# Batched experts MLP: program order on every engine, with the next expert's x cast and transposed between the two layers

## The chip, the cores and the metric

The kernel runs on one core of a Trainium2 chip. The metric is the device time of one execution in microseconds (us). TensorE (PE in the rows, its weight loads PEld) does the matrix products and the transposes, VectorE (DVE) and ScalarE (ACT) move results out of PSUM and cast, GpSimd (POOL) issues the loads of the weights, SyncE (SP) issues the loads of x and the stores of the output. The DMA engines that all these transfers share are shown as "DMA".

## The reference

There are eight experts. Each has its own 256 rows of x, its own first weight matrix and its own second one, all in float32:

```python
n_experts, capacity, hidden, expert_hidden = 8, 256, 512, 2048
x:  (8, 256, 512)    w1: (8, 512, 2048)    w2: (8, 2048, 512)
h = np.matmul(x, w1)
h = np.maximum(h, 0)
return np.matmul(h, w2).astype(np.float32)
```

## The kernel before

Write L1(e) for the first layer of expert e, L2(e) for the second, w1(e) and w2(e) for their weights, T(e) for the cast and transposition of x(e), out(e) for the result. The experts are numbered 0 to 7.

The weights are cast to bfloat16 by the DMA on the way in: each w1(e) and each w2(e) is one tile of 2 MB in SBUF, loaded by one DMA from GpSimd (lines 54 and 60), except that the last, w2(7), comes in four pieces. There are four buffers for w1 and four for w2. A DMA of x(e) (line 50) and one of out(e) (line 117) move 512 KB each and are issued by SyncE; out(7) goes in two halves, one by SyncE (line 114), one by ScalarE (line 115).

T(e) is three steps: ScalarE casts x(e) to bfloat16 (line 64), TensorE does 8 transposes into PSUM (line 68), VectorE copies them to SBUF (line 72). L1(e) is 64 matmuls of 256 columns (line 79) in 8 groups; after each group the ReLU moves the result to SBUF, on ScalarE (line 89) and VectorE (line 87) in turn. L2(e) is 32 matmuls of 512 columns into two PSUM tiles (line 103), then one copy on VectorE (line 111) and one on ScalarE (line 112), and the store.

The program lists the layers in this order, and the weights are requested in the same order: L1(0), L2(0), L1(1), L2(1), ... up to L1(4), L2(4), and then

```python
order += [(1, e) for e in range(E - 3, E)] + [(2, e) for e in range(E - 3, E)]
```

that is L1(5), L1(6), L1(7), L2(5), L2(6), L2(7). T(e) stands at the head of `first_layer(e)`. But what an engine issues first is not taken from this text: the framework's scheduler traces the whole program with its dependencies and buffers, and decides with a model of its own in which order each engine gets its instructions. Each engine then runs its list strictly in order, waiting at an instruction whose inputs are not there.

Of the kernel before, what the change touches and what calls it, by code (L numbers as in the profile page):

```python
# [1 line left out]

# [5 lines left out]


@with_exitstack  # L10
def kernel(
    ctx: ExitStack,
    tc: tile.TileContext,
    x: bass.AP,
    w1: bass.AP,
    w2: bass.AP,
    out: bass.AP,
):
    nc = tc.nc
    P = 128  # L20
    bf = mybir.dt.bfloat16
    f32 = mybir.dt.float32

    E, C, H = x.shape
    F = w1.shape[2]
    MT = C // P
    KT1 = H // P
    KT2 = F // P
    AHEAD = 4


    x_r = x.rearrange("e (p mt) k -> e p mt k", p=P)
    w1_r = w1.rearrange("e (p kt) n -> e p kt n", p=P)
    w2_r = w2.rearrange("e (p kt) n -> e p kt n", p=P)
    out_r = out.rearrange("e (p mt) n -> e p mt n", p=P)

    const = ctx.enter_context(tc.tile_pool(name="const", bufs=1))
    wpool = ctx.enter_context(tc.tile_pool(name="weights", bufs=4))
    xpool = ctx.enter_context(tc.tile_pool(name="xs", bufs=AHEAD))
    tpool = ctx.enter_context(tc.tile_pool(name="xts", bufs=2))  # L40
    hpool = ctx.enter_context(tc.tile_pool(name="hidden", bufs=4))
    opool = ctx.enter_context(tc.tile_pool(name="outs", bufs=3))
    ps_h = ctx.enter_context(tc.tile_pool(name="ps_h", bufs=4, space=bass.MemoryType.PSUM))
    ps_o = ctx.enter_context(tc.tile_pool(name="ps_o", bufs=4, space=bass.MemoryType.PSUM))

    x_sb, w1_sb, w2_sb, ht = {}, {}, {}, {}

    def load_x(e):
        x_sb[e] = xpool.tile([P, MT, H], f32, tag="x", name="x_sb")
        nc.sync.dma_start(x_sb[e][:], x_r[e])  # L50

    def load_w1(e):
        w1_sb[e] = wpool.tile([P, KT1, F], bf, tag="w1", name="w1_sb")
        nc.gpsimd.dma_start(w1_sb[e][:], w1_r[e])  # L54

    def load_w2(e):
        w2_sb[e] = wpool.tile([P, KT2, H], bf, tag="w2", name="w2_sb")
        cuts = (0, KT2) if e < E - 1 else (0, 6, 11, 14, 16)
        for lo, hi in zip(cuts, cuts[1:]):
            nc.gpsimd.dma_start(w2_sb[e][:, lo:hi, :], w2_r[e, :, lo:hi, :])  # L60

    def first_layer(e):
        x_bf = tpool.tile([P, MT, H], bf, tag="xb", name="x_bf")
        nc.scalar.copy(x_bf[:], x_sb[e][:])  # L64
        pt = ps_o.tile([P, KT1, MT, P], bf, tag="ps_o", name="pt_tr")
        for kt in range(KT1):
            for mt in range(MT):
                nc.tensor.transpose(  # L68
                    pt[:, kt, mt, :], x_bf[:, mt, kt::KT1], identity[:]
                )  # L70
        xt = tpool.tile([P, KT1, C], bf, tag="xt", name="xt_sb")
        nc.vector.tensor_copy(xt[:], pt[:].rearrange("p k m q -> p k (m q)"))  # L72

        ht[e] = hpool.tile([P, KT2, C], bf, tag="ht", name="ht_sb")
        for g in range(KT2 // 2):
            ph = ps_h.tile([P, 2, C], f32, tag="ps_h", name="pt_h")
            for i in range(2):
                for kt in range(KT1):
                    nc.tensor.matmul(  # L79
                        ph[:, i, :],  # L80
                        w1_sb[e][:, kt, 2 * g + i::KT2],
                        xt[:, kt, :],
                        start=(kt == 0),
                        stop=(kt == KT1 - 1),
                    )
            if g % 2:
                nc.vector.tensor_relu(ht[e][:, 2 * g:2 * g + 2, :], ph[:])  # L87
            else:
                nc.scalar.activation(  # L89
                    ht[e][:, 2 * g:2 * g + 2, :], ph[:],  # L90
                    mybir.ActivationFunctionType.Relu,
                )

    def second_layer(e):
        last = e == E - 1
        po = [
            ps_o.tile([P, H], f32, tag="ps_o", name=f"pt_o{mt}") for mt in range(MT)
        ]
        order = [(kt, mt) for kt in range(KT2) for mt in range(MT)]
        if last:  # L100
            order = order[:-4] + [(kt, mt) for mt in range(MT) for kt in (KT2 - 2, KT2 - 1)]
        for kt, mt in order:
            nc.tensor.matmul(  # L103
                po[mt][:],
                ht[e][:, kt, mt * P:(mt + 1) * P],
                w2_sb[e][:, kt, :],
                start=(kt == 0),
                stop=(kt == KT2 - 1),
            )
        o = opool.tile([P, MT, H], f32, tag="o", name="out_sb")  # L110
        nc.vector.tensor_copy(o[:, 0, :], po[0][:])  # L111
        nc.scalar.copy(o[:, 1, :], po[1][:])  # L112
        if last:
            nc.sync.dma_start(out_r[e, :, 0, :], o[:, 0, :])
            nc.scalar.dma_start(out_r[e, :, 1, :], o[:, 1, :])
        else:
            nc.sync.dma_start(out_r[e], o[:])


    order = []  # L120
    for e in range(E - 3):
        order += [(1, e), (2, e)]
    order += [(1, e) for e in range(E - 3, E)] + [(2, e) for e in range(E - 3, E)]

    for e in range(AHEAD):
        load_x(e)
    for layer, e in order:
        (load_w1 if layer == 1 else load_w2)(e)
        if (layer, e) == (1, 0):
            identity = const.tile([P, P], bf, name="identity")  # L130
            make_identity(nc, identity)
    for layer, e in order:
        if layer == 1:
            first_layer(e)
        else:
            second_layer(e)
            if e + AHEAD < E:
                load_x(e + AHEAD)


# [1 line left out]
_INS = ['x', 'w1', 'w2']  # L142
_OUTS = [((8, 256, 512), 'float32')]


# [23 lines left out]
```

## Time and profile before

| what | value |
|---|---|
| time, median of 3 runs (lowest to highest) | 193.09 us (192.41 to 193.12) |
| time of the profiled execution | 193.58 us |
| its span, first to last instruction | 191.8 us |
| PE busy | 130.0 us, 68% |
| DVE, ACT, POOL busy | 32.7, 33.0, 10.8 us |
| mean granted TensorE clock | 0.922 |
| HBM read | 71.30 MB, 394 GB/s over the span |

The span runs from the first to the last instruction; the time of the same execution is 1.78 us longer. Times in the rows count from the start of the span. The granted clock is a share of full speed: 1.00 is 2.4 GHz and 0.50 is 1.2 GHz. The largest busy share of an engine, 68%, belongs to PE; the line of the DMA engines has to be read beside it.

### The profile page before, as it was taken

The numbers are of one execution on the slowest core, as the hardware profiler recorded it, in microseconds if no ns is written. First come the engines' busy times: TensorE is split into PE (matmuls) and PEld (weight loads), VectorE is DVE, ScalarE is ACT, GpSimd is POOL, SyncE is SP. The second block draws the span as 40 slices with busy tenths as digits, with TensorE's granted clock in tenths as the row PEclk, the third lists the DMA queues.
The fourth block names the chain that finished last, engine by engine and source line by source line (L and its number), as shares of the span: only waits on it lengthen the run. The fifth ranks groups of instructions, "written<-read, shape, count | busy, mean of one in ns | idle before, by whom it ended". The sixth has DMA issues, their size and how long they took to land.

```text
span 191.8 us, 1891 instructions
## 1 busy us (share of the span) xinstructions
PE 130.0 (68%) x824; PEld 91.5 (48%) x832; DVE 32.7 (17%) x48; ACT 33.0 (17%) x49; POOL 10.8 (6%) x25
## 2 busy tenths in 40 slices
PE   0204969489591978669492956998395029999990
PEld 0103854269240874349341942488385017944440
DVE  0100220203102140204102220053024001301100
ACT  4202220313002220312103220043022001301101
POOL 7200010100100010000301101010000000000000
PEclk9999999969999699969999997899879856999997
DMA  7999999999999999999999899999999999998113
GB/s 253 220 220 259 220 259 222 256 218 260 214 264 214 263 212 263 215 256 221 253 220 262 206 262 222 219 198 256 224 220 215 219 219 219 204 209 212 45 66 111
DMA packets 5192, 42.06 MB, mean 219 GB/s; under 512 B 576, under 2 KB 576, under 8 KB 3264
## 3 DMA queue, kind: packets, MB, share of 16 engines
q0 software_dynamic: 2736, 33.56, 82.4%
q1 hardware_dynamic: 2304, 8.13, 11.2%
q10 hardware_dynamic: 144, 0.26, 0.4%
q8 instruction: 6, 0.10, 0.2%
q14 instruction: 2, 0.02, 0.0%
HBM read 71.30 MB, written 4.19 MB: 394 GB/s over the span
## 4 chain that ended last, share of the span: by engine, by line
PE 54%; DMA 24%; another core or an unknown queue 17%; POOL 1%; issue 1%; DVE 0%; ACT 0%; POOLq 0%; ACTq 0%
PE pt_o L103 27%; PE pt_h L79 26%; DMA w_sb<-in_w_dram 24%; PE pt_tr L68 1%; POOL w_sb L54 0%; DVE xt_sb L72 0%; ACT out_sb L112 0%; POOL w_sb L60 0%; POOL identity masks.py:199 0%; POOL identity masks.py:197 0%; POOLq masks.py:199 0%; ACTq L112 0%; POOLq L153 0%
## 5 line engine op out<-in xcount | busy, mean ns | idle before, releaser
L79 PE MATMUL pt_h<-xt_sb,w_sb 128*128 128x256 bf16 x512 | 67.7, 301 | 29.7 <-DMA w_sb<-in_w_dram 29.4
L79 PEld LDWEIGHTS <-w_sb 128*128 128x128 bf16 x512 | 61.7, 149 | 35.9 <-DMA w_sb<-in_w_dram 30.8
L103 PE MATMUL pt_o<-w_sb,ht_sb 128*128 128x512 bf16 x248 | 58.4, 391 | 22.2 <-DMA w_sb<-in_w_dram 21.6
L103 PEld LDWEIGHTS <-ht_sb 128*128 128x128 bf16 x256 | 25.6, 100 | 52.9 <-issue 25.6
L87 DVE TENSOR_SCALAR ht_sb<-pt_h 128x512 bf16<-128x512 f32 x32 | 22.1, 692 | 87.1 <-PE pt_h L79 87.1
L89 ACT ACTIVATE ht_sb<-pt_h 128x512 bf16<-128x512 f32 x32 | 19.1, 597 | 72.0 <-PE pt_h L79 72.0
L112 ACT COPY out_sb<-pt_o 128x512 f32<-128x512 f32 x8 | 4.7, 586 | 68.7 <-PE pt_o L103 68.7
L111 DVE COPY out_sb<-pt_o 128x512 f32<-128x512 f32 x8 | 5.5, 692 | 61.3 <-PE pt_o L103 61.3
L64 ACT CAST x_bf<-x_sb 128x1024 bf16<-128x1024 f32 x8 | 8.4, 1045 | 13.3 <-DMA x_sb<-in_x_dram 13.3
L54 POOL DMA_DIRECT2D w_sb<-in_w_dram x8 | 4.5, 559 | 77.0 <-PE pt_h L79 76.2
L68 PE MATMUL pt_tr<-identity,x_bf 128*128 128x128 bf16 x64 | 5.1, 231 | 5.1 <-ACT x_bf L64 5.1
L60 POOL DMA_DIRECT2D w_sb<-in_w_dram x11 | 5.9, 542 | 39.0 <-DMA w_sb<-in_w_dram 23.1
L68 PEld LDWEIGHTS <-x_bf 128*128 128x128 bf16 x64 | 4.6, 117 | 6.2 <-ACT x_bf L64 5.1
L72 DVE COPY xt_sb<-pt_tr 128x1024 bf16<-128x1024 bf16 x8 | 5.4, 688 | 6.2 <-PE pt_tr L68 6.2
L64 ACT ACT_TABLE_LOAD x1 | 1.3, 1283 | 0.7 <-PEq L153 0.7
masks.py:199 POOL TENSOR_SCALAR_AFFINE_SELECT identity<-identity 128x128 bf16<-128x128 bf16 x1 | 0.3, 312 | 0.1
masks.py:197 POOL MEMSET identity<- 128x128 bf16 x1 | 0.2, 223 | 0.0
L153 POOL MEMSET const-float32-0.0<- 128x1 f32 x1 | 0.1, 99 | 0.2 <-issue 0.2
L153 POOL MEMSET const-bfloat16-1.0<- 128x1 bf16 x1 | 0.1, 102 | 0.0
L153 POOL MEMSET const-uint8-127<- 128x1 uint8 x1 | 0.1, 102 | 0.0
L153 POOL MEMSET const-float32-1.0<- 128x1 f32 x1 | 0.1, 99 | 0.0
## 6 DMA issues: line engine op xcount, KB each, us to landing
w_sb<-in_w_dram POOLq DMA_DIRECT2D x15, 2048.0 KB, 66.2
x_sb<-in_x_dram SPq DMA_DIRECT2D x8, 512.0 KB, 30.3
out_dram<-out_sb SPq DMA_DIRECT2D x7, 512.0 KB, 15.7
w_sb<-in_w_dram POOLq DMA_DIRECT2D x1, 768.0 KB, 68.2
w_sb<-in_w_dram POOLq DMA_DIRECT2D x1, 640.0 KB, 67.3
w_sb<-in_w_dram POOLq DMA_DIRECT2D x1, 384.0 KB, 58.1
w_sb<-in_w_dram POOLq DMA_DIRECT2D x1, 256.0 KB, 49.6
out_dram<-out_sb SPq DMA_DIRECT2D x1, 256.0 KB, 2.4
```

The lines of the kernel that those rows point to most:

```text
L54: nc.gpsimd.dma_start(w1_sb[e][:], w1_r[e])
L60: nc.gpsimd.dma_start(w2_sb[e][:, lo:hi, :], w2_r[e, :, lo:hi, :])
L64: nc.scalar.copy(x_bf[:], x_sb[e][:])
L68: nc.tensor.transpose(pt[:, kt, mt, :], x_bf[:, mt, kt::KT1], identity[:])
L72: nc.vector.tensor_copy(xt[:], pt[:].rearrange("p k m q -> p k (m q)"))
L79: nc.tensor.matmul(ph[:, i, :], w1_sb[e][:, kt, 2 * g + i::KT2], xt[:, kt, :], start=(kt == 0), stop=(kt == KT1 - 1),)
L87: nc.vector.tensor_relu(ht[e][:, 2 * g:2 * g + 2, :], ph[:])
L89: nc.scalar.activation(ht[e][:, 2 * g:2 * g + 2, :], ph[:], mybir.ActivationFunctionType.Relu,)
L103: nc.tensor.matmul(po[mt][:], ht[e][:, kt, mt * P:(mt + 1) * P], w2_sb[e][:, kt, :], start=(kt == 0), stop=(kt == KT2 - 1),)
L111: nc.vector.tensor_copy(o[:, 0, :], po[0][:])
L112: nc.scalar.copy(o[:, 1, :], po[1][:])
L153: nc = _bacc.Bacc("TRN2", target_bir_lowering=False, num_devices=1)
```

## The change

The scheduler is switched off: with `tc.manual_schedule()` every engine issues its instructions in the order of the program text. T(e) becomes a function of its own, `transpose_x`. It is called for expert 0 before the loop, and for expert e + 1 right behind L1(e). The layers, the loads and the buffers stay as they were.

```diff
-    x_sb, w1_sb, w2_sb, ht = {}, {}, {}, {}
+    x_sb, w1_sb, w2_sb, xt, ht = {}, {}, {}, {}, {}
+    ctx.enter_context(tc.manual_schedule())
...
-    def first_layer(e):
+    def transpose_x(e):
         x_bf = tpool.tile([P, MT, H], bf, tag="xb", name="x_bf")
         nc.scalar.copy(x_bf[:], x_sb[e][:])
...
-        xt = tpool.tile([P, KT1, C], bf, tag="xt", name="xt_sb")
-        nc.vector.tensor_copy(xt[:], pt[:].rearrange("p k m q -> p k (m q)"))
+        xt[e] = tpool.tile([P, KT1, C], bf, tag="xt", name="xt_sb")
+        nc.vector.tensor_copy(xt[e][:], pt[:].rearrange("p k m q -> p k (m q)"))
 
+    def first_layer(e):
         ht[e] = hpool.tile([P, KT2, C], bf, tag="ht", name="ht_sb")
...
+    transpose_x(0)
     for layer, e in order:
         if layer == 1:
             first_layer(e)
+            if e + 1 < E:
+                transpose_x(e + 1)
         else:
             second_layer(e)
             if e + AHEAD < E:
                 load_x(e + AHEAD)
```

On TensorE, near the end of the program, this stood before, behind L1(6). The transposes are those of T(7); `ht_sb_808` and `w2_sb_118` belong to L2(5), `w1_sb_116` is w1(7), so the last rows are the start of L1(7).

```order
L68 LDWEIGHTS x_bf_983
L68 MATMUL pt_tr_985<-identity_89,x_bf_983 128x128
L103 LDWEIGHTS ht_sb_808
L103 MATMUL pt_o0_1077<-w2_sb_118,ht_sb_808 128x512
L103 LDWEIGHTS ht_sb_808
L103 MATMUL pt_o1_1078<-w2_sb_118,ht_sb_808 128x512
...
L103 LDWEIGHTS ht_sb_808
L103 MATMUL pt_o0_1077<-w2_sb_118,ht_sb_808 128x512
L79 LDWEIGHTS w1_sb_116
L79 MATMUL pt_h_997<-xt_sb_994,w1_sb_116 128x256
```

At the same place there now stands this, where `w1_sb_118` is w1(7) and `w2_sb_120` is w2(5):

```order
L71 LDWEIGHTS x_bf_985
L71 MATMUL pt_tr_987<-identity_91,x_bf_985 128x128
L83 LDWEIGHTS w1_sb_118
L83 MATMUL pt_h_999<-xt_sb_996,w1_sb_118 128x256
...
L83 LDWEIGHTS w1_sb_118
L83 MATMUL pt_h_1069<-xt_sb_996,w1_sb_118 128x256
L107 LDWEIGHTS ht_sb_810
L107 MATMUL pt_o0_1079<-w2_sb_120,ht_sb_810 128x512
```

Five matmuls of L2(5) stood ahead of the 64 of L1(7); now all 64 of L1(7) stand ahead of the 32 of L2(5).

On ScalarE, around L2(3), this stood before; the first row is the last ReLU of L1(3), the copy is that of out(3), the cast is x(6), and then come the ReLUs of L1(4):

```order
L89 ACTIVATE ht_sb_542<-pt_h_603 128x512
L112 COPY out_sb_657<-pt_o1_624 128x512
L64 CAST x_bf_889<-x_sb_527 128x1024
L89 ACTIVATE ht_sb_676<-pt_h_677 128x512
L89 ACTIVATE ht_sb_676<-pt_h_697 128x512
```

And now, with the cast of x(4) in place of the cast of x(6):

```order
L93 ACTIVATE ht_sb_544<-pt_h_605 128x512
L67 CAST x_bf_625<-x_sb_274 128x1024
L116 COPY out_sb_672<-pt_o1_639 128x512
L93 ACTIVATE ht_sb_678<-pt_h_679 128x512
L93 ACTIVATE ht_sb_678<-pt_h_699 128x512
```

The cast has moved ahead of the copy of the result, and is that of expert 4 where it was that of expert 6.

On SyncE, the loads of x and the stores of the output; first the list before (-), then the beginning of the list now (+):

```order
-L50 DMA x_sb<-in_x_dram 128x1024 x7
-L117 DMA out_dram<-out_sb 128x1024
-L50 DMA x_sb<-in_x_dram 128x1024
-L117 DMA out_dram<-out_sb 128x1024 x6
-L114 DMA out_dram<-out_sb 128x512
...
+L53 DMA x_sb<-in_x_dram 128x1024 x4
+L121 DMA out_dram<-out_sb 128x1024
+L53 DMA x_sb<-in_x_dram 128x1024
+L121 DMA out_dram<-out_sb 128x1024
+L53 DMA x_sb<-in_x_dram 128x1024
```

Four loads of x stand ahead of the first store instead of seven; x(4) to x(7) now each come behind the store of out(0) to out(3).

## Rows read from the trace of the kernel before

**Rows 1.** The page: DMA's busy tenths in 40 slices; queues with packets, MB, share.

```profile
DMA  7999999999999999999999899999999999998113
q0 software_dynamic: 2736, 33.56, 82.4%
q1 hardware_dynamic: 2304, 8.13, 11.2%
```

**Rows 2.** Waits of PE for weights: us in total, times, longest.

```profile
PE pt_h L79 <- DMA w_sb<-in_w_dram: 29.4, 6, 10.9
PE pt_o L103 <- DMA w_sb<-in_w_dram: 21.6, 6, 10.0
```

**Rows 3.** The chain that ended last: start, duration, what; its last part.

```profile
146.70 9.99 another core or an unknown queue
...
157.53 1.49 PE pt_o L103 x3
159.02 8.41 PE pt_h L79 x64
...
167.49 10.74 PE pt_o L103 x49
...
178.28 8.81 PE pt_o L103 x40
...
187.16 0.58 ACT out_sb L112
```

**Rows 4.** Timeline, TensorE: start, duration, instruction, [idle before and its releaser].

```profile
72.36 7.07 PE L103 MATMUL pt_o<-w_sb,ht_sb 128*128 128x512 bf16 x31 [1.48 <-DMA w_sb<-in_w_dram]
...
83.38 8.79 PE L79 MATMUL pt_h<-xt_sb,w_sb 128*128 128x256 bf16 x64 [3.51 <-DMA w_sb<-in_w_dram]
...
94.52 7.07 PE L103 MATMUL pt_o<-w_sb,ht_sb 128*128 128x512 bf16 x31 [2.35 <-DMA w_sb<-in_w_dram]
...
105.54 7.21 PE L79 MATMUL pt_h<-xt_sb,w_sb 128*128 128x256 bf16 x64 [3.51 <-DMA w_sb<-in_w_dram]
...
116.58 8.75 PE L103 MATMUL pt_o<-w_sb,ht_sb 128*128 128x512 bf16 x31 [3.82 <-DMA w_sb<-in_w_dram]
...
126.36 7.11 PEld L79 LDWEIGHTS <-w_sb 128*128 128x128 bf16 x64 [0.29 <-DMA w_sb<-in_w_dram]
...
137.38 8.88 PE L79 MATMUL pt_h<-xt_sb,w_sb 128*128 128x256 bf16 x64 [3.67 <-DMA w_sb<-in_w_dram]
...
156.73 0.59 PE L103 MATMUL pt_o<-w_sb,ht_sb 128*128 128x512 bf16 x1 [10.03 <-DMA w_sb<-in_w_dram]
```

**Rows 5.** Windows of 1 us: length, busy by engine, clock, DMA share, GB/s.

```profile
175.00:176.00 1.00, 1.00 (x6) 0.48 (x5) 0.00 (x0) 0.00 (x0) 0.00 (x0) 1.00 1.03 350
176.00:177.00 1.00, 1.00 (x7) 0.41 (x6) 0.00 (x0) 0.00 (x0) 0.00 (x0) 1.00 0.41 168
```

**Rows 6.** Timeline, ScalarE and VectorE, around the end of L1(6).

```profile
145.41 0.60 ACT L89 ACTIVATE ht_sb<-pt_h 128x512 bf16<-128x512 f32 x1 [1.15 <-PE pt_h L79]
...
146.89 0.68 DVE L72 COPY xt_sb<-pt_tr 128x1024 bf16<-128x1024 bf16 x1
```

**Rows 7.** The page's groups: busy, mean ns of one | idle before.

```profile
L64 ACT CAST x_bf<-x_sb 128x1024 bf16<-128x1024 f32 x8 | 8.4, 1045 | 13.3 <-DMA x_sb<-in_x_dram 13.3
L68 PE MATMUL pt_tr<-identity,x_bf 128*128 128x128 bf16 x64 | 5.1, 231 | 5.1 <-ACT x_bf L64 5.1
```

**Rows 8.** Windows of 2 us, columns as above, across the long wait.

```profile
150.00:152.00 2.00, 0.00 (x0) 0.00 (x0) 0.00 (x0) 0.00 (x0) 0.00 (x0) 0.89 1.11 238
152.00:154.00 2.00, 0.00 (x0) 0.00 (x0) 0.00 (x0) 0.00 (x0) 0.00 (x0) 0.50 1.11 238
...
162.00:164.00 2.00, 2.00 (x21) 2.00 (x20) 0.71 (x2) 0.60 (x1) 0.00 (x0) 1.00 1.19 254
```

**Rows 9.** Timeline of SyncE, first issues of x.

```profile
0.74 18.12 SPq L50 DMA_DIRECT2D x_sb<-in_x_dram  x7
```

**Rows 10.** Loads of x, from issue to landing.

```profile
DMA to landing us min/median/max: 3.3/30.3/46.8
```

More of the change, by code (lines that the diff above doesn't have):

```diff
@@ L81, in first_layer @@
                         w1_sb[e][:, kt, 2 * g + i::KT2],
-                        xt[:, kt, :],
+                        xt[e][:, kt, :],
                         start=(kt == 0),
```

## The prediction

> **What bounds the kernel now.** I began with the DMA line of the page, not with the busy shares. It is at eight tenths or more from the second slice to the 37th of 40, and falls off in the last three, 15 us [rows 1]; PE at 68% is not what limits that stretch. The waits say it from the other side: PE's long waits are all for weights, 29.4 us in L1 and 21.6 us in L2 [rows 2]. So for most of the run the kernel goes at the pace of the stream of weights, and what TensorE does earlier or later there is given back at the next wait. The place that is different is the end. The last weights have landed at about 176.4 us (the DMA share is 1.03 in the microsecond from 175 and 0.41 in the next) [rows 5], but the chain of waits runs on without a pause through PE: 1.49, 8.41, 10.74 and 8.81 us, to 187.1 us [rows 3]. From 156.7 us on the bound is TensorE, about 10.7 us behind the stream. Ahead of that the chain has a hole of 9.99 us [rows 3], and the timeline says what it is: the first matmul of L2(5) at 156.73 us, after 10.03 us of waiting for weights [rows 4].
>
> **Which weights TensorE waited for.** The stream is one queue in program order, so landings can be counted along it. L1 and L2 that began on a landing did so at 105.54 (w1(4)), 116.58 (w2(4)), 126.36 (w1(5)), 137.38 (w1(6)) and 156.73 us (w2(5)) [rows 4]. The steps are 11.04, 9.78, 11.02 and 19.35 us. The last step holds two tiles, w1(7) and w2(5), so 9.68 us each, and w1(7) landed near 137.38 + 9.68 = 147.1 us. In the same way w2(6) and w2(7) fill the time from 156.73 to 176.4 us, 9.83 us each, so w2(6) landed near 166.6 us. TensorE was thus waiting from 146.7 us for w2(5), with w1(7) in SBUF from about 147.1 us, because the scheduler had put five matmuls of L2(5) ahead of the 64 of L1(7).
>
> **The change at the end of the program.** Now L1(7) stands ahead of all of L2(5). Step by step:
> - T(7) must be done first. Its cast stands behind the last ReLU of L1(6) on ScalarE, which ended at 146.01 us [rows 6]. The cast takes 1.05 us and 8 transposes 0.6 us (the rows of page groups give 231 ns for one, but they overlap: eight took 0.45 us on the chain, and I allow 0.6) [rows 7], the copy 0.68 us [rows 6]: 148.4 us, 1.3 us after w1(7).
> - L1(7) takes 7.21 us at full clock and up to 8.88 us where the clock was down at its start [rows 4]: it ends between 155.6 and 157.3 us. Before, it ran from 159.0 to 167.4 us.
> - L2(5) starts at the landing of w2(5), 156.73, or at 157.3 us. A second layer with full clock takes 7.07 us [rows 4]: it ends at 163.8 to 164.4 us.
> - L2(6) waits for w2(6): 166.6 us, and a little more, since out(5) now leaves at about 165 us, while weights still come. I add 0.2 us.
> - L2(6) and L2(7) are 64 matmuls. In the last stretch 49 took 10.74 us and 40 took 8.81 us [rows 3], 0.22 us each: 64 x 0.22 = 14.1 us. The end of PE is then 166.8 + 14.1 = 180.9 us, against 187.1.
> - What follows (0.58 us of copy [rows 3] and the last store, 4.7 us up to the end of the span) stays.
>
> So the span loses 6.2 us and the profiled execution goes from 193.58 to 187.4 us. The median of the runs shown is 0.49 us under the profiled one: 186.9 us.
>
> **Are the weights there for L2(7)?** Its last four matmuls would start 60 x 0.22 = 13.2 us after 166.8, at 180.0 us. Without other traffic the weights end at 176.4 us. The steps above give the price of a store or a load of x in the stream: 11.04 and 11.02 against 9.78 us [rows 4], so 1.25 us for 512 KB beside the weights; the queue's share gives 11.2% of 191.8 us over 15.5 such tiles, 1.39 us [rows 1]. out(5) and, if it leaves by 175 us, out(6) now fall into the stream: 176.4 + 2 x 1.39 = 179.2 us. That is 0.8 us before 180.0, so TensorE stays the bound. The Trainium skill bears on this ("DMA: Bandwidth & Descriptors", Queues, rings and completion order): each DMA engine takes turns between the queues that have work, packet by packet. By that rule a new store doesn't line up behind the weights but takes its share at once; were it served behind them, the weights would end at 176.4 us and the margin would be 3.6 us. The steps of 11.0 us agree with the rule.
>
> **The rest of the change.** In the steady part T(e+1) moves from behind L2(e) to ahead of it. There it costs TensorE 0.6 us, ScalarE 1.05 us, and a wait: the transposes can't start until the cast is done, and all of L2(e) is queued behind them. Behind the end of L1 that is about 1.4 us until L2 may start. It is covered where w2(e) lands later than that: the waits ahead of L2 are 1.48 us (the shortest of those shown), 2.35 and 3.82 us [rows 4]. If the cover is gone, L2 starts late by 0 to 0.6 us, and that comes off the wait ahead of the next L1, 3.51 us in two rows [rows 4]. On the end it is 0 by both bounds, and I take 0. Behind L2(e), the transposes leave the gap in front of L1(e+1); that gains nothing, as w1(e+1) is what L1 waits for, except 0.2 us at L1(5), which is given back at w1(6).
>
> On SyncE four loads of x instead of seven go out at the start, where seven took 18 us until the last was issued [rows 9]; x(4) to x(7) follow later, each behind a store. The bytes are the same and all of them land before w1(6), so the landing of w1(6) and all behind it stay (bounds: one tile of x early or late, 1.25 us either way at a landing in the middle, 0 at 137.4 us). The identity now stands ahead of the load of w2(0): half a microsecond, hidden as w1(0) still occupies the queue.
>
> **The rivals.**
> - *The clock falls in the wait ahead of L2(6).* Between L2(5) and w2(6) TensorE idles for 2.2 to 2.8 us. The rows: 2.35 us of idleness before an L2 cost nothing (7.07 us), 3.82 us made it 8.75 us; 3.51 us made L1 8.79 us at one place and left it at 7.21 us at another [rows 4]. In the long wait the clock was 0.89 and then 0.50 from about 4 us on, and 1.00 again at 162 us [rows 8]. Price 8.75 - 7.07 = 1.7 us, all of it on the end: 188.6 us. The nearest row by length is 2.35 us, without a loss, so this isn't the likeliest. Beside it stands the Trainium skill ("TensorE: Matmul & The Clock Gate", Part 1): the low clock is the default and activity releases it. By that rule the end, with matmuls from 148 us on and only short gaps, should run at full clock more than before; the trace agrees as to the long wait, and is undecided at 2.8 us.
> - *The stream is the bound after all.* If each of the two stores costs twice the 1.25 us of the steps, the weights end at 181.4 us, and 4 x 0.22 us of matmuls later PE ends at 182.3 us: 188.3 us, with a wait of L2(7) for its last piece. Against it: no step of the rows with one such transfer in it is longer than 11.04 us.
> - *No gain: w1(7) isn't there.* No instruction of the trace waited for w1(7) alone. If it lands only with w2(5) at 156.7 us, L1(7) ends at 163.9 to 165.6 us and 96 matmuls x 0.22 = 21.1 us later PE ends at 185.0 to 186.7 us: 191.0 to 192.7 us. Against it: one queue, and equal steps between the landings that the trace shows.
> - *Slower: the casts wait for late x.* ScalarE and TensorE issue in order, so a late x(e+1) now stops out(e)'s copy and all of L2(e), and at the end L1(7) with everything behind it. x(7) is now issued behind out(3), near 102 us (L2(3) began at 94.52 us and took 7.07 us [rows 4]), and needed at 146 us. The longest time from issue to landing was 46.8 us [rows 10], which would be 149 us, 3 us late and within the slack of L2(5). PE would end after 187.1 us only if L1(7) ended after 187.1 - 21.1 = 166 us, so if x(7) came after 156.5 us (T(7) and L1(7) take 2.3 and 7.2 us), 54.5 us from issue. From there each us costs one: 60 us in flight would make 199 us. With two requests at a time on that queue instead of seven I expect less than the median of 30.3 us [rows 10].
>
> **How the numbers follow.** The forecast, 186.9 us, has a chance of 0.60; the clock rival, 188.6, 0.28; the stream rival, 188.3, 0.07; no gain 0.03; slower 0.02. Both ends of the range: 186.9 less 0.7 us of spread between the runs before and 0.8 us for a landing of w2(6) that I worked out and did not see, 185.4 us; the clock rival plus 0.8 us for the same, 189.4 us. The other two lie above it and make 0.05. A difference under 0.5%, about 1 us, can't be told from no change here. Faster 0.95, the same 0.03, slower 0.02.
>
> **What would show it.** Right: L1(7) starts between 147 and 149 us, with no wait of 10 us anywhere after 20 us; L2(5) starts near 156.7 us; a wait of 2 to 3 us ahead of L2(6); then 64 matmuls of L2 in about 14.1 us; DMA busy until 178 to 179 us instead of 176.4. L2(6) over 8 us shows the clock rival, a wait inside L2(7) the stream rival. In the steady part the landings of w2(e) should not move by more than about 1.3 us. The prediction is wrong in its core if L1(7) starts after 150 us, or if weights end later than 180 us.

## The result and the profile after

The changed kernel took 186.76 us (median of 4 runs, 186.63 to 187.47) against 192.75 us before (4 runs, 192.36 to 193.12). The ratio is 0.9697, with a 95% interval from 0.9662 to 0.9732. In a later comparison on one chip six more runs gave 186.69 to 188.63 us, median 187.77, with a ratio of 0.9727 (0.9685 to 0.9768); that they fall into two groups is a part of what follows. The forecast was 186.9 us and faster.

The profiled execution took 186.63 us, its span is 184.9 us. Waits of PE for weights after, as us in total, times, longest; they answer to [rows 2]:

```profile
PE pt_h L83 <- DMA w_sb<-in_w_dram: 31.4, 7, 10.3
PE pt_o L107 <- DMA w_sb<-in_w_dram: 7.9, 6, 2.6
```

L1 waits about as long as before, 2.0 us more in all. The waits of L2 have shrunk from 21.6 to 7.9 us, and their longest from 10.0 to 2.6 us: the long one is gone and no other has taken its place. The chain that ended last in the changed kernel, its last part (start, duration, what), answers to [rows 3]:

```profile
145.60 1.05 ACT x_bf L67
...
146.69 0.65 PE pt_tr L71 x8
...
147.37 0.70 DVE xt_sb L75
...
148.11 7.15 PE pt_h L83 x64
155.26 1.17 another core or an unknown queue
...
156.90 6.64 PE pt_o L107 x30
163.53 2.60 another core or an unknown queue
...
166.17 4.26 PE pt_o L107 x19
...
170.49 9.68 PE pt_o L107 x44
...
180.22 0.69 DVE out_sb L115
```

Read it from the top. T(7) is on the chain and finishes at 148.1 us; L1(7) follows at once, where before the chain had its hole of 9.99 us; two short waits for w2(5) and w2(6); then L2(6) and L2(7) without a pause to 180.2 us. Timeline of TensorE in the changed kernel, with the idle time before each row and its releaser; it answers to [rows 4]:

```profile
104.01 8.68 PE L83 MATMUL pt_h<-xt_sb,w_sb 128*128 128x256 bf16 x64 [3.92 <-DMA w_sb<-in_w_dram]
...
115.46 7.07 PE L107 MATMUL pt_o<-w_sb,ht_sb 128*128 128x512 bf16 x31 [1.38 <-DMA w_sb<-in_w_dram]
...
126.03 7.21 PE L83 MATMUL pt_h<-xt_sb,w_sb 128*128 128x256 bf16 x64 [3.50 <-DMA w_sb<-in_w_dram]
...
137.07 8.87 PE L83 MATMUL pt_h<-xt_sb,w_sb 128*128 128x256 bf16 x64 [2.45 <-DMA w_sb<-in_w_dram]
...
148.11 7.15 PE L83 MATMUL pt_h<-xt_sb,w_sb 128*128 128x256 bf16 x64 [0.78 <-DVE xt_sb L75]
...
156.47 7.07 PE L107 MATMUL pt_o<-w_sb,ht_sb 128*128 128x512 bf16 x31 [1.21 <-DMA w_sb<-in_w_dram]
...
166.17 13.97 PE L107 MATMUL pt_o<-w_sb,ht_sb 128*128 128x512 bf16 x63 [2.64 <-DMA w_sb<-in_w_dram]
```

The row of 148.11 was released by VectorE's copy of T(7), not by the DMA: w1(7) was there by then, as worked out (147.1 us). The landings of w1(6) and w2(5), at 137.07 and 156.47 us, are 0.3 us from those of before, so at the end of the program the stream of weights is as before. And the windows of 1 us at the end of the stream (the column before the last is the DMA share), which answer to [rows 5]:

```profile
176.00:177.00 1.00, 1.00 (x7) 0.43 (x5) 0.00 (x0) 0.00 (x0) 0.00 (x0) 1.00 1.00 330
177.00:178.00 1.00, 1.00 (x6) 0.45 (x5) 0.00 (x0) 0.00 (x0) 0.00 (x0) 1.00 0.40 164
```

The stream, with out(5) and out(6) in it, ends near 177.4 us, 1 us later than before.

### The profile page after: what moved, and what is told of

Its sections match the earlier page's. It is cut to its first block, busy times and chain, and to the rows that moved or that the text cites. A ratio compares the mean times of both kernels' runs of the same rounds, so it can differ in the third digit from the quotient of the medians.

```text
span 184.9 us, 1887 instructions
## 1 busy us (share of the span) xinstructions
PE 129.4 (70%) x825; PEld 90.4 (49%) x832; DVE 33.2 (18%) x48; ACT 32.6 (18%) x49; POOL 10.9 (6%) x25
## 4 chain that ended last, share of the span: by engine, by line
PE 53%; DMA 25%; another core or an unknown queue 13%; ACT 3%; issue 2%; POOL 1%; DVE 1%; ACTq 0%; POOLq 0%
PE pt_o L107 27%; DMA w_sb<-in_w_dram 25%; PE pt_h L83 24%; ACT x_bf L67 3%; PE pt_tr L71 2%; POOL w_sb L57 1%; DVE xt_sb L75 0%; DVE out_sb L115 0%; POOL w_sb L63 0%; POOL identity masks.py:199 0%; POOL identity masks.py:197 0%; ACT ht_sb L93 0%; ACTq L116 0%; POOLq masks.py:199 0%
## 5 line engine op out<-in xcount | busy, mean ns | idle before, releaser
L107 PE MATMUL pt_o<-w_sb,ht_sb 128*128 128x512 bf16 x249 | 56.0, 379 | 8.3 <-DMA w_sb<-in_w_dram 7.9
L107 PEld LDWEIGHTS <-ht_sb 128*128 128x128 bf16 x256 | 25.0, 98 | 37.5 <-issue 8.8
L71 PEld LDWEIGHTS <-x_bf 128*128 128x128 bf16 x64 | 4.1, 118 | 11.9 <-ACT x_bf L67 11.9
```

Of the source, the lines that this page charges most:

```text
L71: nc.tensor.transpose(pt[:, kt, mt, :], x_bf[:, mt, kt::KT1], identity[:])
L107: nc.tensor.matmul(po[mt][:], ht[e][:, kt, mt * P:(mt + 1) * P], w2_sb[e][:, kt, :], start=(kt == 0), stop=(kt == KT2 - 1),)
```

## The experiments

The theory: all of the gain is that L1(7) now stands ahead of L2(5) on TensorE. The rivals: the new place of T brings a part of it; the scheduler's absence brings a part elsewhere. Then come the terms at the end of the program: the wait ahead of L2(6), the stores in the stream, and the clock. Runs of one comparison share the chip and its runs of before: the first four stand against 193.27 us.

**T back at the head of L1(e), in program order.**

```diff
-    transpose_x(0)
...
+            transpose_x(e)
             first_layer(e)
-            if e + 1 < E:
-                transpose_x(e + 1)
```

> Program order on every engine, but T(e) back at the head of L1(e), where the program text of before has it. Theory (all of the gain is L1(7) standing ahead of L2(5) on TensorE): the end of the program is the same as in the changed kernel, so 186.8 us, L1(7) starting near 148 us and L2(6) near 166 us. In the steady part cast, transposes and copy stand behind L2(e) again, some 2.4 us, and L1(e+1) may start a few tenths later than its weights; the next wait takes that back. Rival (a part of the gain is the new place of T): the time lies clearly above the changed kernel's, at 188 to 192.7 us.

Measured: 187.35 us (186.58 to 188.37), ratio 0.9688 (0.9638 to 0.9738). Two of the four runs are at 186.6 us, as the changed kernel, two at 188.1 and 188.4 us. The place of T isn't the difference: the profiled run is the one at 188.37 us, and there L1(7) started at 146.9 us, 1.2 us earlier than in the profiled run of the changed kernel. Its end of TensorE's timeline, and windows of 2 us with the granted clock in the third column from the right:

```profile
157.05 7.07 PE L107 MATMUL pt_o<-w_sb,ht_sb 128*128 128x512 bf16 x32 [2.94 <-DMA w_sb<-in_w_dram]
166.30 15.66 PE L107 MATMUL pt_o<-w_sb,ht_sb 128*128 128x512 bf16 x64 [2.19 <-DMA w_sb<-in_w_dram]
```

```profile
164.00:166.00 2.00, 0.11 (x1) 0.00 (x0) 0.63 (x1) 0.59 (x1) 0.00 (x0) 1.00 0.83 172
166.00:168.00 2.00, 1.70 (x5) 0.58 (x5) 0.00 (x0) 0.00 (x0) 0.00 (x0) 0.58 1.04 215
168.00:170.00 2.00, 2.00 (x7) 0.76 (x6) 0.00 (x0) 0.00 (x0) 0.00 (x0) 0.57 0.98 262
```

The clock was 1.00 through most of the wait for w2(6) and fell as the wait ended: the mean of 0.58 from 166 to 168 us leaves it 0.3 us at full speed there. It was back by 170 us, and the 64 matmuls took 15.66 us instead of 13.97: 1.69 us, all of it on the end. That is the clock rival with its price of 1.7 us, in a kernel whose order at the end is that of the changed one.

**T between the layers, the scheduler on.**

```diff
-    ctx.enter_context(tc.manual_schedule())
```

> T(e+1) called behind L1(e) as in the changed kernel, but the framework's scheduler left on. On TensorE it puts T between the layers as in the changed kernel, and again five matmuls of L2(5) ahead of L1(7). Theory: PE waits about 10 us for w2(5) with w1(7) already there, L1(7) starts near 158.5 us, and the time is that of before, 192.5 to 193 us. Rival (the new place of T brings the gain): 187 to 190 us.

Measured: 200.06 us (199.65 to 200.87), ratio 1.0348 (1.0312 to 1.0383): slower than before by 7 us. The expectation had the order wrong. With T in its new place the scheduler puts only three matmuls of L2(5) first, but ahead of L1(6) and L1(7) both. TensorE's timeline at the end, and three rows at the beginning of the same run:

```profile
156.80 1.44 PE L106 MATMUL pt_o<-w_sb,ht_sb 128*128 128x512 bf16 x3 [22.26 <-DMA w_sb<-in_w_dram]
...
158.03 16.30 PE L82 MATMUL pt_h<-xt_sb,w_sb 128*128 128x256 bf16 x128
```

```profile
28.66 1.04 ACT L66 CAST x_bf<-x_sb 128x1024 bf16<-128x1024 f32 x1 [9.93 <-DMA x_sb<-in_x_dram]
29.61 1.08 ACT L92 ACTIVATE ht_sb<-pt_h 128x512 bf16<-128x512 f32 x2
30.25 6.53 PE L82 MATMUL pt_h<-xt_sb,w_sb 128*128 128x256 bf16 x32 [7.16 <-ACT ht_sb L92]
```

The wait for w2(5) is 22.26 us long, with w1(6) and w1(7), which by the order of the queue landed ahead of w2(5), unused meanwhile, and 128 matmuls of L1 follow it. So T moved alone, with the scheduler on, is a loss. What the place of T is worth by itself this run can't tell, since the scheduler's order changed with it; the first run tells it: with T back in its old place the time is that of the changed kernel. The second fence shows the mechanism of the slower rival of the prediction in another place: a cast put early on ScalarE waited 9.93 us for x, two ReLUs queued behind it, and L1(0) stood still for 7.16 us. Later waits for the stream took that back.

**One thing undone: five matmuls of L2(5) ahead of L1(7).**

```diff
+            if e == E - 1:
+                second_layer(E - 3, 0, 5)
             first_layer(e)
...
-            second_layer(e)
+            second_layer(e, 5 if e == E - 3 else 0)
```

(`second_layer` takes the range of its matmuls; the rest is the changed kernel.)

> The changed kernel with one thing undone: five matmuls of L2(5) are written ahead of L1(7), everything else in program order with T between the layers. Theory: 192.3 to 192.8 us, with a wait of about 9.5 us ahead of the first of the five, at 147 to 156.5 us, and TensorE busy from there to the end near 187 us. Rival (switching the scheduler off brings the gain elsewhere, by the loads of x that come later or by other waits): under 190 us.

Measured: 193.12 us (10 runs, 192.4 to 193.89), ratio 0.9998 (0.9968 to 1.0029). The chain, from the end of T(7):

```profile
145.07 0.64 PE pt_tr L71 x8
145.71 10.86 another core or an unknown queue
...
156.61 2.29 PE pt_o L111 x5
158.90 7.83 PE pt_h L83 x64
166.73 19.65 PE pt_o L111 x91
```

Five matmuls, 2.3 us of work at the granted clock of 0.50 to which the wait had brought it down (1.1 us at full clock), in front of 64 that could have run: the hole is back, at 10.86 us, and so is the whole time of before. Everything else in the change, the scheduler's absence, the later loads of x and the place of T, makes no difference that this shows.

**w2(6) in four pieces.**

```diff
-        cuts = (0, KT2) if e < E - 1 else (0, 6, 11, 14, 16)
+        cuts = (0, KT2) if e < E - 2 else (0, 6, 11, 14, 16)
```

> The changed kernel with w2(6) loaded in the same four pieces as w2(7) (6, 5, 3 and 2 sixteenths). Theory (the end of TensorE is the landing of all of w2(6) plus 64 matmuls): L2(6) starts on its first piece, right behind L2(5) near 163.5 us, instead of waiting until 166.2; then the stream is the bound: the last piece of w2(7) at about 177.7 us and four matmuls, PE ends near 178.7 instead of 180.2 us. Time 1.3 to 2 us under the changed kernel, 184.8 to 185.5 us. Rival (the stream of weights, slowed by the two stores, sets the end already): no change, within 0.5 us of 186.8, with waits inside L2(7).

Measured: 186.4 us (185.94 to 186.69), ratio 0.9634 (0.9607 to 0.9661). Less gain than expected, though the wait ahead of L2(6) was gone. L2(7) waited for its pieces instead; its last rows on TensorE and the landing that released the end in the chain:

```profile
171.34 2.76 PE L107 MATMUL pt_o<-w_sb,ht_sb 128*128 128x512 bf16 x12 [0.40 <-DMA w_sb<-in_w_dram]
174.83 2.32 PE L107 MATMUL pt_o<-w_sb,ht_sb 128*128 128x512 bf16 x10 [0.73 <-DMA w_sb<-in_w_dram]
177.73 2.54 PE L107 MATMUL pt_o<-w_sb,ht_sb 128*128 128x512 bf16 x10 [0.58 <-DMA w_sb<-in_w_dram]
```

```profile
157.20 22.00 DMA w_sb<-in_w_dram
...
179.25 1.04 PE pt_o L107 x4
```

The last piece came at 179.2 us, not at the 177.7 that I had expected. L2(6) ended earlier, so out(6) left near 171.9 us instead of 173.9 and lay in the stream as a whole. With both stores, at 1.25 us each, the 176.4 us of before become 178.9. The stream is the bound here; the next runs try that.

The next three runs, and the one with nine idle matmuls, stand against 192.94 us; the changed kernel beside them is the one with 187.77 us. The other two stand against 193.46 us.

**The changed kernel again.**

> The changed kernel as it is, as the base for the three runs beside it. Theory: 186.6 to 187 us in most runs; where the clock falls in the wait ahead of L2(6), 1.7 us more, 188.1 to 188.6 us, at a lower mean clock. Rival (the clock has no part here): all runs within 0.5 us.

Measured: 186.69, 186.74, 187.01, 188.52, 188.62 and 188.63 us. Two groups, 1.8 us apart; nothing lies between. The mean clock is 0.918 in each of the three longer ones and 0.923 to 0.947 in the others. That fits the clock rival but doesn't show it: none of the three was profiled, and the mean over the span is a weak sign, as the run of 187.47 us in the first comparison has 0.911.

**out(5) and out(6) behind the weights.** GpSimd requests them, in the queue that carries the weights.

```diff
-            nc.sync.dma_start(out_r[e], o[:])
+            (nc.gpsimd if e >= E - 3 else nc.sync).dma_start(out_r[e], o[:])
```

> The changed kernel with out(5) and out(6) requested by GpSimd, so that they stand in the same queue behind the last weights and take nothing from them. Theory (TensorE is the bound from the landing of w2(6) on): PE still ends near 180.2 us, the weights end 1 to 2.5 us earlier, near 176.0 us, and the time stays within 0.5 us of the changed kernel. Rival (the last weights, slowed by the two stores, set the end): 1 to 2 us less.

Measured: 186.76 us (186.61 to 188.05), ratio 0.969 (0.9659 to 0.9721); the profiled run, at 186.79 us, has the same 13.97 us of L2 at the end as the changed kernel. The last piece of w2(7) is requested at 126.3 to 126.6 us in the kernel before, in the changed kernel and here; in this order, its time from issue to landing (the last column, in us):

```profile
w_sb<-in_w_dram POOLq DMA_DIRECT2D x1, 256.0 KB, 49.6
w_sb<-in_w_dram POOLq DMA_DIRECT2D x1, 256.0 KB, 51.0
w_sb<-in_w_dram POOLq DMA_DIRECT2D x1, 256.0 KB, 49.7
```

So the weights end 1 us earlier again, and the time doesn't follow. Without another change the stores cost nothing: TensorE was the bound after w2(6), as the prediction had it.

**Both: w2(5) and w2(6) in pieces, the stores behind.** The edit is the two above, with `e < E - 3` in the cuts.

> The changed kernel with both: w2(5) and w2(6) in the same four pieces as w2(7), and out(5) and out(6) behind the last weights in the same queue. Theory: TensorE runs from 148 us without a wait until L2(7) catches up with the stream; the last piece lands near 176 to 176.7 us and four matmuls later, near 177.5 us, PE ends, 2.7 us before the changed kernel. The two stores then run beside the halves of out(7) and cost up to 1 us of that: 184 to 185 us. Rival (pieces make the stream itself slower, as the last piece at 179.2 us in the run with w2(6) in pieces might mean): 186 to 187 us.

Measured: 184.23 us (184.1 to 185.37), ratio 0.9558 (0.9526 to 0.9589). It beats both kernels. TensorE's timeline at the end:

```profile
154.44 13.98 PE L107 MATMUL pt_o<-w_sb,ht_sb 128*128 128x512 bf16 x62
170.29 2.76 PE L107 MATMUL pt_o<-w_sb,ht_sb 128*128 128x512 bf16 x12 [1.88 <-DMA w_sb<-in_w_dram]
173.37 4.48 PE L107 MATMUL pt_o<-w_sb,ht_sb 128*128 128x512 bf16 x20 [0.31 <-DMA w_sb<-in_w_dram]
```

L2(5) and L2(6) run in one piece from L1(7) on, and the last 20 matmuls without a wait to 177.85 us: the last piece was there by 177 us, 2 us earlier than with the stores in the stream. PE ends 2.3 us before the 180.2 of the changed kernel.

**w2(6) alone in pieces, the stores behind.** The cuts of the fourth run, with out(5) and out(6) behind the weights as in the sixth.

> The changed kernel with w2(6) in four pieces and out(5), out(6) behind the last weights in the same queue; w2(5) stays one transfer. It asks why w2(6) in pieces alone gave so little: there the last piece landed at 179.2 us, not at 177.7. Theory (an earlier L2(6) sent out(6) into the stream earlier too, so that both stores lay ahead of the last piece): with the stores behind the weights L2(6) starts near 164 us, the last piece lands by 177 us, PE ends near 178 us, and the time is 184.3 to 185 us. Rival (the pieces themselves slow the stream): the last piece again near 179 us, 186 to 186.5 us.

Measured: 184.83 us, ratio 0.9582 (0.9536 to 0.9629), again in two groups: 183.90, 183.97 and 184.00, and 185.66, 185.81 and 185.88 us. The lower group settles the question of the fourth run, from which this one differs by the stores alone. There the last piece came at 179.2 us; here the profiled run, of 184.00 us, does L2(5), L2(6) and L2(7) in one stretch to 177.7 us:

```profile
156.68 21.02 PE L107 MATMUL pt_o<-w_sb,ht_sb 128*128 128x512 bf16 x94 [0.81 <-DMA w_sb<-in_w_dram]
```

The pieces don't slow the stream; the stores did. Its upper group is 1.8 us above the lower, and why isn't shown: there is no profile of a run of it, and its mean clock, 0.935 to 0.944, is not lower than that of the lower group, 0.923 to 0.934. One wait is left here, ahead of L2(5), with no slack behind it, so a fall of the clock there would come out on the end. With w2(5) in pieces too (184.1 to 184.28 us in five of six runs, 185.37 us in one) that wait is gone.

**Work in the wait ahead of L2(6).** Nine idle matmuls, whose result nobody reads; in the comparison with the changed kernel's six runs.

```diff
+    fill = {E - 2: 9}
...
+            if e in fill:
+                ph = ps_h.tile([P, 2, C], f32, tag="ps_h", name="pt_fill")
+                for _ in range(fill[e]):
+                    nc.tensor.matmul(
+                        ph[:], ht[e][:, 0, :P], w2_sb[E - 4][:, 0, :],
+                        start=True, stop=True,
+                    )
             second_layer(e)
```

> The changed kernel with nine matmuls of 512 columns, whose result nobody reads, between L2(5) and L2(6), so that TensorE works through 2 of the 2.6 us in which it waits for w2(6). Theory (the clock falls in that wait in some runs, and then costs 1.7 us): all runs at 186.5 to 187 us, none at 188 or more. Rival (the scatter of the changed kernel comes from the stream): the same scatter as the changed kernel beside it.

Measured: 187.3 us (186.61 to 188.21), ratio 0.9708 (0.9676 to 0.974). Inconclusive: 188.21, 187.73 and 187.64 us remain, and none of these was profiled. A possible reason: nine matmuls are 2 us at full clock, and where L2(5) itself runs with a fallen clock they are pushed past the landing of w2(6). The profile of the changed kernel's second comparison (186.74 us) shows that L2(5) can be late so; here are its rows, and its windows of 2 us at the start of L2(5):

```profile
157.01 0.59 PE L107 MATMUL pt_o<-w_sb,ht_sb 128*128 128x512 bf16 x1 [2.91 <-DMA w_sb<-in_w_dram]
157.82 7.92 PE L107 MATMUL pt_o<-w_sb,ht_sb 128*128 128x512 bf16 x30 [0.22 <-issue]
166.31 13.97 PE L107 MATMUL pt_o<-w_sb,ht_sb 128*128 128x512 bf16 x63 [0.57 <-DMA w_sb<-in_w_dram]
```

```profile
156.00:158.00 2.00, 0.77 (x2) 0.41 (x3) 0.00 (x0) 0.00 (x0) 0.00 (x0) 0.75 0.96 205
158.00:160.00 2.00, 2.00 (x6) 0.65 (x5) 0.00 (x0) 0.00 (x0) 0.00 (x0) 0.50 1.23 262
```

The clock fell as the wait ahead of L2(5) ended (the mean of 0.75 is one microsecond at either level), L2(5) took 8.73 us, from 157.01 to 165.74, instead of 7.07, the extra 1.7 us went into the wait ahead of L2(6), and the time stayed at 186.7 us. Behind such an L2(5) nine matmuls would end near 167.7 us, 1.4 us after w2(6) came. So the next run breaks both waits, with less work in each.

```diff
-    fill = {E - 2: 9}
+    fill = {E - 3: 5, E - 2: 5}
```

> The changed kernel with five idle matmuls of 512 columns, whose result nobody reads, ahead of L2(5) and five ahead of L2(6), 1.1 us each at full clock, so that the two waits are broken and yet nothing is pushed past the landings of w2(5) and w2(6). Theory (the runs at 188.5 us are those in which the clock falls in one of these waits): all runs at 186.5 to 187.2 us. Rival (other causes, or short fillers don't hold the clock): runs near 188.5 us remain.

Measured: 186.74, 186.76, 186.79, 186.79, 186.86 and 187.35 us, ratio 0.9677 (0.9648 to 0.9707). No run lies near 188.5 us, and five of the six lie within 0.12 us. That is what the theory expected, but six runs don't prove it: the first four runs of the changed kernel had no such run either, and over its ten runs three were long. If it holds, work that does nothing, 1.1 us of it in each wait, saves the 1.8 us of those runs.

## Why the prediction was right, point by point

- **What bounds it.** Right. [rows 2 to 4] named the hole ahead of L2(5) and what it held back; undoing the order alone gave the 193 us back.
- **w1(7) in SBUF from 147.1 us.** Right: VectorE's copy released L1(7), not the weights, and with T(7) done earlier L1(7) began at 146.9 us.
- **The terms.** T(7) done at 148.1 us (148.4 worked out, from terms that add up to 148.3), L1(7) 7.15 us (7.21), L2(5) from 156.47 to 163.53 us (156.73 to 163.8), the wait for w2(6) to 166.17 us (166.8), the 64 matmuls 14.0 us (14.1), PE's end 180.2 us (180.9), the rest 4.7 us. The 0.7 us between is 0.3 us of an earlier landing of w2(5), 0.1 us since w2(6) came 9.70 instead of 9.83 us behind it, the 0.2 us that I had added for out(5) and that did not show, and 0.1 us of the matmuls. That the median came within 0.2 us of the forecast is luck in part: the end worked out was 0.7 us late, and the 0.49 us taken off because the median before lay under the profiled run hid most of that; now the median lies 0.13 us above the profiled run.
- **Are the weights there.** The sign was right, the size was not. The stores moved the end of the stream by 1.0 us, not by 2.8: the prediction charged both in full, but out(6) left at 173.9 us, near its end. The fourth run shows what they cost when both lie in it, 179.2 us; taking them out was worth nothing to the changed kernel and some 2 us to that one (186.4 us with them; without them 184.0 in the lower group, 184.83 as a median). Stores from SyncE delay the weights in these runs, the same stores behind them in their own queue don't, as the prediction had it.
- **The steady part.** Nothing on the end, as said; the landings moved a little more than the 1.3 us that I allowed (w2(3) at 93.02 instead of 94.52 us, 1.5 us) and are back within 0.3 us at w1(6). The later requests of x(4) to x(7) are the likely reason; no run tests that alone.
- **The rivals.** "No gain" and "slower" did not happen: the longest load of x took 26.4 us to land. The clock rival very likely did, in three of the ten runs of the changed kernel, so its chance of 0.28 was about right; that none was among the first four is luck. Price and time are those forecast (1.7 worked out, 1.69 us in the profile of T's old place, 1.8 us between the groups; 188.6 us), but the long runs of the changed kernel itself were not profiled. The prediction looked for a fall only ahead of L2(6); in the second profile it comes ahead of L2(5), where the wait behind it takes it up. My reading of it by the length of the wait was wrong: 2.64 us left the clock up in one run, 2.19 us in the run of T's old place brought it down.

## What to carry to other kernels

Where a stream of loads sets the pace, count its landings along the queue and look for an engine that waits for a late tile while an earlier one lies unused: five matmuls in the wrong place of a queue that issues in order held back all the work behind them and cost 6 us here. A scheduler's order is an input to be read like the rest, since moving one function with the scheduler on made it worse by 7 us. And once the order is right, the last tiles in pieces and the stores behind the loads in the same queue take the next 2.5 us (186.76 to 184.23), where pieces of w2(6) alone gave a part of it and the stores alone nothing.

## What had not been expected of the hardware

One kernel on one core has two times, 186.7 and 188.6 us. In the one long run that was profiled (T's old place, 188.37 us) the difference is TensorE's clock, which fell to its lower level at the end of a wait of 2.19 us; that the other long runs have the same cause is likely and not shown. Beside the rows above, the changed kernel has 64 matmuls of L1 in 7.21 us after a wait of 3.50 us and in 8.87 us after one of 2.45 us: in these rows the length of a wait alone doesn't tell whether it costs.
